# Compact state space tables in five parts and a held latent normalization in a two-layer hybrid decoder trunk

## The chip, the cores and the metric

The kernel runs on one core of a Trainium2 chip. The metric is the device time of one execution in microseconds (us); lower is better. PE is TensorE (matmul), DVE is VectorE, ACT is ScalarE, POOL is GpSimd, and SP is SyncE, whose queue issues nearly all DMAs.

## The reference, cut to what matters

Two layers work on one sequence of 256 tokens with 1024 features, in float32. Each layer runs three token mixers on the same input x and joins them with gates: an RWKV-7 time mix, a latent attention (MLA), and a diagonal state space mixer (S5). Then come an output projection, a layer norm, a SwiGLU feed-forward network (FFN), and a second layer norm.

```python
p = x @ w_in[l]
y_a = rwkv7_time_mix(p[..., :o_mla], ...)
y_b = mla_branch(p[..., o_mla:o_s5], ...)
y_c = s5_branch(p[..., o_s5:o_gate], ...)
merged = gates[..., 0, :] * y_a + gates[..., 1, :] * y_b + gates[..., 2, :] * y_c
x = layer_norm(ALPHA * x + merged @ w_out[l], ...)
h = silu(x @ ffn_w1[l]) * (x @ ffn_w3[l])
x = layer_norm(ALPHA * x + h @ ffn_w2[l], ...)
```

Two pieces matter here. The S5 mixer has 32 groups with 64 complex states and 16 channels each. From `lambda` and `log_step` it derives a magnitude, a cosine and a sine per state, and multiplies the input matrices B by a complex factor f:

```python
mag, ang = jnp.exp(lam_re * step), lam_im * step
lb_re, lb_im = mag * jnp.cos(ang), mag * jnp.sin(ang)
bb_re = f_re[..., None] * br - f_im[..., None] * bi
bb_im = f_re[..., None] * bi + f_im[..., None] * br
```

The MLA branch normalizes two latent vectors (256 and 128 wide) by their root mean square before it projects them up.

## The kernel before, in words

**Weights.** There are 138 weight chunks of 128x1024 floats per layer, in the order in which they are used. For each chunk `w_load` issues one DMA on SP's queue into a ring of 3 buffers (`raw`), ACT casts it to the fp32r value `whi` (L161), and DVE subtracts to get the rest `wlo` (L171; a tail of some chunks is subtracted on POOL, L173). Each product is then three matmuls, `whi` with the high part of x, `whi` with its low part, `wlo` with the high part (L203 to L205). `w_next` runs four chunks ahead; `whi` and `wlo` have four buffers each.

**Order of the work.** `ORDER1` and `ORDER2` spell out each layer's mixer stage as tokens. In `ORDER1[0]`: `S0 S1` project the S5 input, `m` the MLA latents, `P` loads the layer's parameters, `r0` to `r6` are seven RWKV projections (`rw_unit`, two chunks and 48 matmuls each, with a shift of tokens in `mix_in`: ACT at L570, DVE at L571), `G1` to `G3` gates, `T0 T1 T2` the three parts of the state space tables, `N` the normalization of the latents (`mla_norm`), `t`/`w` the two halves of four S5 tiles, `g0 g1` their gelu. The tokens give the program order, which is a priority and not the order in which instructions are issued. When the program is built, a planner goes through it with its own costs: for each engine it takes, of the instructions that it reckons to be ready, the one that stands first in the program. So a late instruction that is ready early goes ahead of an earlier one. On the chip each engine and SP's queue then work strictly in the order so fixed.

**State space tables** (`s5_tables`, a generator; each token advances it to the next `yield`). First come the scalars of both layers (`s5scal`, on DVE with two sines on ACT). `exp_acc` computes an exponential by a polynomial with 24 instructions on 128x32 values, and is called twice, in a chain. Then:

- Part one loads B and C, padded with zeros to block diagonal 128x512 matrices by the host (two DMAs of 512 KB), and makes three complex products with `cmul` (L381 to L386, six 128x512 instructions each) and one negation (L394). In layer 0 all of it is on DVE, in layer 1 on POOL.
- Part two transposes `bd` on PE (L404) and makes the small matrix `k0` (L413).
- Part three is the rotation: cosine and sine tables `ct`, `st` for 128 steps, by doubling (L429 to L434), 48 instructions of 128x16 to 128x512, on POOL in both layers. It reads and writes SBUF alone.

The S5 tiles need all of it: `bl` for the matmul at L702, `ct` and `st` for DVE's L709 and L710, `m2` for the scans (L721), `k0` and `cd` for L735 to L747.

**Latents.** `mla_norm` takes squares on ACT with a sum (L624, L625), adds epsilon on DVE (L235), takes the power -0.5 on POOL (L237, tile `rsm`), scales `lt` on ACT (L630, L631), rotates a part on DVE (L635 to L638), transposes on PE (L643 to L649) and copies to `mlain` on ACT (L645, L650). Nothing reads `mlain` before token `U` of `ORDER2`. The copies of the S5 input `u` (L113) are on ACT too, and eight DMAs on SP's queue bring them to `U2` (L671).

**Layer 1's tables** are made during layer 0's FFN: the loop over f = 2..21 advances the generator at f in `TAB_AT = (7, 12, 17)`, in a temporary pool `tmp1`. After the last part the pool's memory goes to the layer norm's `lg`, `lb` and `xk`, whose loads (L493 to L495) stand on SP's queue among the weight loads.

Of the kernel before, what the change touches and what calls it, by code (L numbers as in the profile page):

```python
# [8 lines left out]
F32 = mybir.dt.float32  # L9
# [17 lines left out]
    "S0 m S1 P r0 T0 T1 r1 N T2 r2 t0 w0 r3 G3 t1 t2 w1 r4 r5 w2 t3 w3 g0 G1 r6 G2 g1",  # L27
# [6 lines left out]
TAB_AT = (7, 12, 17)  # L34
# [52 lines left out]
def trunk(ctx: ExitStack, tc: tile.TileContext, xT, xtok, ws, spA, spB, spC, sp5, lnv, cst, out, dbg=None,  # L87
# [112 lines left out]

    def mm3(ps, w, x, first, last):
# [67 lines left out]
    with tc.tile_pool(name="s5set", bufs=1) as q:  # L269
# [5 lines left out]
        def exp_acc(dst, src):  # L275
            xc, n, r, pl = t5("xc"), t5("n"), t5("r"), t5("pl")
            ni = t5("ni", I32)
            V.tensor_scalar(out=xc, in0=src, scalar1=-104.0, scalar2=88.7, op0=ALU.max, op1=ALU.min)
# [13 lines left out]
            V.tensor_tensor(out=dst, in0=pl, in1=ni.bitcast(F32), op=ALU.mult)  # L292
# [55 lines left out]
    def s5_tables(l, tab, tmp, G, E):  # L348
# [12 lines left out]
        pb = tmp.tile([128, 2, 8, 2, 32], F32, name="pb", tag="pb")  # L361
        SY.dma_start(out=pb, in_=spB[l, :, 0:1024].rearrange("p (r q a c) -> p r q a c", r=2, q=8, a=2))
# [25 lines left out]
        def B(i, ri):
            return bd[:, :, ri, :, i]

        cmul(B(1, 0), B(1, 1), s5fr[:, p0:p0 + 16], s5fi[:, p0:p0 + 16], pb[:, 0], pb[:, 1])
        cmul(B(0, 0), B(0, 1), lr, li, B(1, 0), B(1, 1))

        G.tensor_scalar(out=cd[:, 1], in0=cd[:, 1], scalar1=-1.0, scalar2=None, op0=ALU.mult)  # L394
        G.tensor_scalar(out=li, in0=li, scalar1=-1.0, scalar2=None, op0=ALU.mult)
        cmul(cd[:, 2], cd[:, 3], lr, li, cd[:, 0], cd[:, 1])
# [123 lines left out]
    for l in range(layers):  # L520
# [136 lines left out]
        with tc.tile_pool(name=f"s5p{l}", bufs=1, side=P) as q:  # L657
# [17 lines left out]
            def s5_tables0(i):  # L675
# [4 lines left out]
                if i == 2:  # L680
                    tgen[0][0].close()
# [807 lines left out]
```

## Time and profile before

| | |
|---|---|
| time, median of 3 runs | 1086.61 us (1079.62 to 1089.05) |
| profiled execution | 1090.58 us, its span 1088.9 us |
| PE busy | 1026.9 us (94%) |
| DVE busy | 802.8 us (74%) |
| ACT busy | 477.3 us (44%) |
| POOL busy | 231.5 us (21%) |
| mean granted TensorE clock | 0.972 of full speed |

The trace is of one execution. Times are from the start of the span. The matmuls' ends are modelled, so a PE that is shown busy need not be at its peak. In a list of instructions a line gives start, duration, engine, line, operation and tile, and in brackets the idle time of the engine before it and what ended that.

### The profile page before, as it was taken

Reading aid. Unit: us, or ns where it says so; the run is one execution under the profiler, and the core shown is the slowest. Engines: PE = TensorE matmul, PEld = TensorE weight load, DVE = VectorE, ACT = ScalarE, POOL = GpSimd, SP = SyncE. Lnnn points to the kernel's source line nnn. Section 1 sums busy time; section 2 is a strip of 40 time slices with the busy share of each in tenths; the row PEclk is TensorE's granted clock in tenths of the full one; section 3 lists DMA queues with packets and bytes.
Section 4 is the critical chain, followed back from the end, with each engine's and each line's share of the span. In section 5 each row is a group of like instructions: output and inputs, shape, how many; then the busy total and the mean of one; then the engine's idle time right before and its main releaser. Section 6 shows DMA issues by size and latency. Waiting matters only on the chain.

```text
span 1088.9 us, 21216 instructions
## 1 busy us (share of the span) xinstructions
PE 1026.9 (94%) x8560; PEld 923.8 (85%) x8560; DVE 802.8 (74%) x1560; ACT 477.3 (44%) x789; POOL 231.5 (21%) x254
## 2 busy tenths in 40 slices
PE   9489999999999999899998999999999899999997
PEld 8378887888897899798878999878889779999985
DVE  7599988977478799576473898789756866676645
ACT  5243387544343344244325345765334433434331
POOL 2941042210000599400011003221002420000000
PEclk9789999999999999999998899999999999999999
DMA  7342262132285655466545325222225746555552
GB/s 279 98 140 86 95 192 73 59 118 96 81 291 183 204 173 167 178 209 217 184 143 177 115 80 173 90 97 79 79 98 169 243 152 230 186 183 180 186 195 78
DMA packets 47683, 164.91 MB, mean 151 GB/s; under 512 B 5729, under 2 KB 8289, under 8 KB 46689
## 3 DMA queue, kind: packets, MB, share of 16 engines
q1 hardware_dynamic: 47296, 163.03, 45.2%
q8 instruction: 67, 1.10, 0.4%
q10 hardware_dynamic: 288, 0.52, 0.1%
q14 instruction: 32, 0.25, 0.1%
HBM read 157.77 MB, written 4.19 MB: 149 GB/s over the span
## 4 chain that ended last, share of the span: by engine, by line
PE 61%; DVE 17%; POOL 10%; DMA 5%; ACT 3%; issue 3%; SPq 0%; DVEq 0%; ACTq 0%; POOLq 0%
PE mm L205 11%; PE mm L204 11%; PE mm L203 11%; DMA raw<-in_ws 4%; PE mm L488 3%; PE mm L489 3%; PE mm L487 3%; DVE wlo L171 3%; ACT whi L161 2%; DVE z L721 2%; POOL st L432 1%; POOL st L434 1%; PE pa L702 1%; POOL t L430 1%; PE pa L916 1%
## 5 line engine op out<-in xcount | busy, mean ns | idle before, releaser
L171 DVE TENSOR_TENSOR wlo<-raw,whi 128x1024 fp32r<-128x1024 f32 (+2 forms) x265 | 336.7, 1277 | 175.3 <-ACT whi L161 173.2
L161 ACT CAST whi<-raw 128x1024 fp32r<-128x1024 f32 (+2 forms) x267 | 277.5, 1043 | 386.0 <-PE mm L204 207.3
L203 PE MATMUL mm<-xh,whi 128*128 128x256 f32 x1312 | 379.5, 289 | 14.2 <-ACT whi L161 14.1
L205 PE MATMUL mm<-xh,wlo 128*128 128x256 f32 x1312 | 378.3, 289 | 2.1 <-DVE wlo L171 1.9
L204 PE MATMUL mm<-xl,whi 128*128 128x256 f32 x1312 | 379.3, 289 | 0.4 <-DVE xl L259 0.4
L203 PEld LDWEIGHTS mm<-xh,whi 128*128 128x128 f32 x1312 | 252.5, 192 | 18.7 <-ACT whi L161 14.7
L205 PEld LDWEIGHTS mm<-xh,wlo 128*128 128x128 f32 x1312 | 253.5, 193 | 6.1 <-DVE wlo L171 2.9
L204 PEld LDWEIGHTS mm<-xl,whi 128*128 128x128 f32 x1312 | 252.4, 192 | 3.9 <-issue 1.8
L237 POOL TENSOR_TENSOR rs<-rs,mhalf 128x1 f32<-128x1 f32 x8 | 7.8, 970 | 344.0 <-DVE rs L235 344.0
L203 PE MATMUL mm<-yh,whi 128*128 128x256 f32 x256 | 74.5, 291 | 0.1
L205 PE MATMUL mm<-yh,wlo 128*128 128x256 f32 x256 | 74.1, 290 | 0.0
L204 PE MATMUL mm<-yl,whi 128*128 128x256 f32 x256 | 74.1, 289 | 0.0
L488 PE MATMUL mm<-wlo,hh 128*128 128x512 f32 x132 | 52.0, 394 | 0.0
L487 PE MATMUL mm<-whi,hh 128*128 128x512 f32 x132 | 51.6, 394 | 0.0
L489 PE MATMUL mm<-whi,hl 128*128 128x512 f32 x132 | 51.5, 393 | 0.0
L203 PEld LDWEIGHTS mm<-yh,whi 128*128 128x128 f32 x256 | 48.5, 189 | 2.3 <-ACT qa L113 0.9
L204 PEld LDWEIGHTS mm<-yl,whi 128*128 128x128 f32 x256 | 48.5, 189 | 1.2 <-issue 0.8
L205 PEld LDWEIGHTS mm<-yh,wlo 128*128 128x128 f32 x256 | 48.6, 190 | 1.1 <-issue 0.7
L173 POOL TENSOR_TENSOR wlo<-raw,whi 128x384 fp32r<-128x384 f32 (+2 forms) x24 | 29.5, 1236 | 72.4 <-ACT whi L161 72.4
L237 POOL TENSOR_TENSOR rsn<-rsn,mhalf 128x8 f32<-128x8 f32 x4 | 6.5, 1634 | 142.8 <-DVE rsn L235 142.8
L923 POOL TENSOR_SCALAR_AFFINE_SELECT Mk<-Mk 64x512 f32<-64x512 f32 x32 | 27.0, 844 | 43.6 <-ACT Mk L113 42.3
L487 PEld LDWEIGHTS mm<-whi,hh 128*128 128x128 f32 x132 | 24.8, 188 | 6.1 <-DVE th L1260 0.7
(498 smaller groups left out, 1764.2 us busy)
## 6 DMA issues: line engine op xcount, KB each, us to landing
raw<-in_ws SPq DMA_DIRECT2D x267, 512.0 KB, 4.1
raw<-in_ws SPq DMA_DIRECT2D x8, 416.0 KB, 3.5
xd<-xk SPq DMA_DIRECT2D x3, 1024.0 KB, 4.1
xk<-xd SPq DMA_DIRECT2D x3, 1024.0 KB, 7.9
lg<-in_lnv SPq DMA_DIRECT2D x4, 512.0 KB, 5.1
lb<-in_lnv SPq DMA_DIRECT2D x4, 512.0 KB, 5.7
pc<-in_spC SPq DMA_DIRECT2D x2, 768.0 KB, 5.1
pb<-in_spB SPq DMA_DIRECT2D x2, 512.0 KB, 5.2
```

Source lines behind the costliest of these rows:

```text
L161: S.copy(out=hi[:, s], in_=raw[:, s])
L171: V.tensor_tensor(out=lo[:, 0:m], in0=raw[:, 0:m], in1=hi[:, 0:m].bitcast(F32), op=ALU.subtract)
L173: G.tensor_tensor(out=lo[:, m:w], in0=raw[:, m:w], in1=hi[:, m:w].bitcast(F32), op=ALU.subtract)
L203: PE.matmul(ps, lhsT=wh, rhs=xh, start=first, stop=False)
L204: PE.matmul(ps, lhsT=wh, rhs=xl, start=False, stop=False)
L205: PE.matmul(ps, lhsT=wl, rhs=xh, start=False, stop=last)
L237: G.tensor_tensor(out=out, in0=in_, in1=mh(out), op=ALU.pow)
L487: PE.matmul(acc[b][n], lhsT=ah, rhs=w[0][:, s], start=(k == 0), stop=False)
L488: PE.matmul(acc[b][n], lhsT=ah, rhs=w[1][:, s], start=False, stop=False)
L489: PE.matmul(acc[b][n], lhsT=al, rhs=w[0][:, s], start=False, stop=(k == nk - 1))
L721: V.tensor_tensor_scan(out=z[:, pp, qq, ri], data0=bc(m2[:, j:j + 1], [128, 128]), data1=z[:, pp, qq, ri], initial=0.0, op0=ALU.mult, op1= ...
L923: G.affine_select(out=Mk[r, h], in_=Mk[r, h], pattern=[[0, 4], [1, 2], [1, 64]], compare_op=ALU.is_ge, fill=0.0, base=-1, channel_multipli ...
```

## The change

The host no longer pads B and C; one DMA of 512 KB brings all four compact matrices. `cmul` works on them in place with 128x256 instructions, two at a time on separate scratch tiles, and a new step `spread` writes the padded form with two instructions of 128x512 output each (mask columns `g0`, `g1`): on ACT in layer 0, on POOL in layer 1. There are four spreads, so eight such instructions per layer. In layer 0 the tables come in five parts, the rotation first, and the tokens move: the products that need the tables go behind `r3`, the normalization `N` goes behind `r5`, and an order on ScalarE keeps its four squares behind the last `mix_in` activation traced before it, that of `r5`. In layer 1 the parts are advanced at f = 7, 8, 9, 12, 17, the rotation last. `exp_acc` needs 15 instructions in place of 24.

```diff
-    "S0 m S1 P r0 T0 T1 r1 N T2 r2 t0 w0 r3 G3 t1 t2 w1 r4 r5 w2 t3 w3 g0 G1 r6 G2 g1",
+    "S0 m S1 P r0 T0 T1 r1 T2 T3 r2 r3 T4 G3 t0 w0 r4 t1 r5 N w1 t2 w2 r6 t3 w3 g0 G1 G2 g1",
-TAB_AT = (7, 12, 17)
+TAB_AT = (7, 8, 9, 12, 17)
...
-            V.tensor_scalar(out=n, in0=n, scalar1=MAGIC, scalar2=None, op0=ALU.subtract)
-            V.tensor_scalar(out=n, in0=n, scalar1=-127.0, scalar2=127.0, op0=ALU.max, op1=ALU.min)
+            V.tensor_scalar(out=n, in0=n, scalar1=MAGIC + 127.0, scalar2=MAGIC, op0=ALU.min, op1=ALU.subtract)
...
-            for k in range(6, -1, -1):
-                V.tensor_tensor(out=pl, in0=pl, in1=r, op=ALU.mult)
-                V.tensor_scalar(out=pl, in0=pl, scalar1=co[k], scalar2=None, op0=ALU.add)
+            for k in range(7, 0, -1):
+                V.scalar_tensor_tensor(out=pl, in0=pl, scalar=co[k], in1=r, op0=ALU.add, op1=ALU.mult)
...
-        SY.dma_start(out=pb, in_=spB[l, :, 0:1024].rearrange("p (r q a c) -> p r q a c", r=2, q=8, a=2))
+        SY.dma_start(out=pb, in_=spB[l].rearrange("p (r q a c) -> p r q a c", r=4, q=8, a=2))
...
+        if first:
+            rotation()
+            yield
+        bt, bs = (tmp.tile([128, 8, 2, 16], F32, name=n, tag=n) for n in ("bt", "bs"))
...
+        def cmul(x, fr, fi):
+            fr, fi = (bc(v2(t, 8).unsqueeze(3), [128, 8, 2, 16]) for t in (fr, fi))
+            G.tensor_tensor(out=bs, in0=x[:, 0], in1=fi, op=ALU.mult)
+            G.tensor_tensor(out=bt, in0=x[:, 1], in1=fi, op=ALU.mult)
+            G.tensor_tensor(out=x[:, 0], in0=x[:, 0], in1=fr, op=ALU.mult)
+            G.tensor_tensor(out=x[:, 1], in0=x[:, 1], in1=fr, op=ALU.mult)
+            G.tensor_tensor(out=x[:, 0], in0=x[:, 0], in1=bt, op=ALU.subtract)
+            G.tensor_tensor(out=x[:, 1], in0=x[:, 1], in1=bs, op=ALU.add)
+        def spread(dst, src):
+            for g in range(2):
+                o, i = dst[:, :, 16 * g:16 * g + 16], src.rearrange("p r q a c -> p (r q a) c")
+                if l:
+                    G.tensor_scalar(out=o, in0=i, scalar1=C(f"g{g}"), scalar2=None, op0=ALU.mult)
+                else:
+                    S.activation(out=o, in_=i, func=AF.Identity, scale=C(f"g{g}"))
+        cmul(pb[:, 0:2], s5fr[:, p0:p0 + 16], s5fi[:, p0:p0 + 16])
+        spread(bdv[:, :, 1], pb[:, 0:2])
+        G.tensor_scalar(out=pb[:, 3], in0=pb[:, 3], scalar1=-1.0, scalar2=None, op0=ALU.mult)
+        spread(cd[:, 0:2].rearrange("p r q a c -> p (r q a) c"), pb[:, 2:4])
+        yield
+        cmul(pb[:, 0:2], lr, li)
+        spread(bdv[:, :, 0], pb[:, 0:2])
+        yield
+        G.tensor_scalar(out=li, in0=li, scalar1=-1.0, scalar2=None, op0=ALU.mult)
+        cmul(pb[:, 2:4], lr, li)
+        spread(cd[:, 2:4].rearrange("p r q a c -> p (r q a) c"), pb[:, 2:4])
+        yield
...
-            S.activation(out=dst, in_=ps, func=AF.Identity, scale=omu[:, col:col + 1])
+            state["mix"] = S.activation(out=dst, in_=ps, func=AF.Identity, scale=omu[:, col:col + 1])
...
+            with tc.issue_after(inst(state["mix"])) if l == 0 else ExitStack():
+                for b in range(2):
+                    S.activation(out=sq, in_=lt[:, b, 0:256], func=AF.Square, scale=1.0 / 16, accum_out=ss[:, b, 0:1])
...
```

## Rows read from the trace of the kernel before

**Rows 1.** Busy time by stretches: PE, PEld, DVE, ACT, POOL, PEclk, DMA share, GB/s.
```profile
20.00:30.00 10.00, 9.61 (x66) 9.39 (x65) 9.86 (x55) 6.75 (x16) 5.96 (x13) 1.00 0.77 257
...
33.90:46.20 12.30, 3.09 (x26) 2.88 (x24) 0.29 (x2) 1.73 (x4) 11.83 (x18) 0.77 0.01 6
...
36.99:80.00 43.01, 22.26 (x200) 21.05 (x200) 32.70 (x32) 16.19 (x29) 30.23 (x24) 0.72 0.31 94
...
46.20:79.00 32.80, 21.26 (x188) 20.05 (x189) 32.51 (x31) 13.46 (x26) 21.27 (x14) 0.72 0.38 115
79.00:145.00 66.00, 62.85 (x705) 56.74 (x703) 62.79 (x125) 29.26 (x44) 11.12 (x9) 1.00 0.35 114
145.00:200.00 55.00, 54.33 (x381) 46.75 (x382) 46.21 (x138) 41.70 (x99) 13.72 (x21) 1.00 0.31 99
```

**Rows 2.** Waits of PE, 0 to 160 us: total, times, longest.
```profile
PE mm L203 <- ACT whi L161: 9.5, 2, 9.3
PE pb L413 <- DVE bd L383: 7.3, 1, 7.3
```

**Rows 3.** Instructions of ACT, of POOL and of DVE around the first wait.
```profile
44.47 0.51 ACT L630 ACTIVATE lt<-lt,rsm 128x256 f32<-128x256 f32 x1 [14.56 <-POOL rsm L237]
...
43.39 1.04 POOL L237 TENSOR_TENSOR rsm<-rsm,mhalf 128x4 f32<-128x4 f32 x1
...
46.23 1.66 DVE L171 TENSOR_TENSOR wlo<-raw,whi 128x1024 fp32r<-128x1024 f32 x1 [12.04 <-ACT whi L161]
```

**Rows 4.** Waits of SP's queue, in layer 0 and in layer 1: total, times, longest.
```profile
SPq L671 <- ACT lt L630: 17.0, 1, 17.0
...
SPq L493 <- POOL st L434: 12.1, 1, 12.1
```

**Rows 5.** DVE instructions: a product beside the rotation, one alone, two 128x256 alone.
```profile
63.49 1.75 DVE L384 TENSOR_TENSOR bd<-bd,lr 128x512 f32<-128x512 f32 x1
...
71.89 0.68 DVE L382 TENSOR_TENSOR bt<-cd,li 128x512 f32<-128x512 f32 x1
...
99.82 0.42 DVE L711 TENSOR_TENSOR z<-pa__1092,pb__1093 128x256 f32<-128x256 f32 x1
100.15 0.42 DVE L712 TENSOR_TENSOR z<-pa__1092,pb__1093 128x256 f32<-128x256 f32 x1
```

**Rows 6.** POOL instructions of the rotation: one alone, and the same form beside DVE.
```profile
41.36 1.04 POOL L430 TENSOR_TENSOR t<-st 128x512 f32<-128x512 f32 x1
...
52.53 1.51 POOL L430 TENSOR_TENSOR t<-st 128x512 f32<-128x512 f32 x1
```

**Rows 7.** PE in layer 1: the gap behind SP's wait, and the clock after it.
```profile
460.12 0.46 PE L203 MATMUL mm<-xh,whi 128*128 128x256 f32 x1 [4.54 <-ACT whi L161]
...
460.00:468.00 8.00, 7.30 (x36) 7.01 (x37) 7.57 (x12) 4.25 (x7) 0.00 (x0) 0.57 0.53 178
```

**Rows 8.** Busy time of DVE and POOL where both work, after that wait.
```profile
46.80:67.90 21.10, 9.61 (x107) 8.59 (x106) 21.10 (x17) 5.14 (x9) 20.67 (x14) 0.66 0.33 100
```

**Rows 9.** ACT: an Identity of 128x512 between SBUF tiles.
```profile
135.60 0.72 ACT L762 ACTIVATE ga<-ga,ones 128x512 f32<-128x512 f32 x1
```

**Rows 10.** DVE groups, 10 to 34 us (mean ns of one after the comma): half of the polynomial of `exp_acc`.
```profile
L289 DVE TENSOR_TENSOR t5pl<-t5pl,t5r 128x32 f32<-128x32 f32 x14 | 2.8, 197 | 0.2
```

**Rows 11.** POOL in layer 1: 128x256 steps (first, last), products (first, last), rotation's end, negation.
```profile
380.14 0.61 POOL L429 TENSOR_TENSOR ct<-ct 128x256 f32<-128x256 f32 x1
...
382.80 1.10 POOL L381 TENSOR_TENSOR bd<-pb,s5fr 128x512 f32<-128x512 f32 x1
...
414.33 1.73 POOL L434 TENSOR_TENSOR st<-st,t 128x256 f32<-128x256 f32 x1
...
419.12 1.47 POOL L386 TENSOR_TENSOR cd<-cd,bt 128x512 f32<-128x512 f32 x1
...
447.12 2.15 POOL L434 TENSOR_TENSOR st<-st,t 128x512 f32<-128x512 f32 x1
...
L394 POOL TENSOR_SCALAR cd<-cd 128x512 f32<-128x512 f32 x1 | 1.5, 1547 | 0.0
```

More of the change, by code (lines that the diff above doesn't have):

```diff
@@ L346, in step, with s5_tables @@
             next(g)
-    def s5_tables(l, tab, tmp, G, E):
+    def s5_tables(l, tab, tmp, G, E, first):
         mark("s5pre")
@@ L388, in B, with rotation @@
[L388 to L394, printed above, removed]
+        def rotation():
+            mark("s5pre")
+            t2 = tmp.tile([128, 16, 32], F32, name="t2", tag="t2")
+            n = 1
+            while n < 128:
+                w = min(n, 32)
+                lc, ls = (bc(x[:, :, n - 1:n], [128, 16, w]) for x in (ct, st))
+                for o in range(0, n, w):
+                    c0, s0, t = ct[:, :, o:o + w], st[:, :, o:o + w], t2[:, :, 0:w]
+                    c1, s1 = ct[:, :, n + o:n + o + w], st[:, :, n + o:n + o + w]
+                    E.tensor_tensor(out=c1, in0=c0, in1=lc, op=ALU.mult)
+                    E.tensor_tensor(out=t, in0=s0, in1=ls, op=ALU.mult)
+                    E.tensor_tensor(out=c1, in0=c1, in1=t, op=ALU.subtract)
+                    E.tensor_tensor(out=s1, in0=c0, in1=ls, op=ALU.mult)
+                    E.tensor_tensor(out=t, in0=s0, in1=lc, op=ALU.mult)
+                    E.tensor_tensor(out=s1, in0=s1, in1=t, op=ALU.add)
+                n *= 2
@@ L412, in s5_tables @@
             for ri in range(2):
[L413 removed]
+                PE.matmul(o, lhsT=bd[:, ri, qx, pp, 1], rhs=cd[:, ri, qx, pp], start=(ri == 0), stop=(ri == 1),
                           skip_group_check=True)
@@ L417, in s5_tables @@
             cp(1, out=k0[r], in_=v2(ps[r, 0:256], 8))
-        yield
-        mark("s5pre")
-        t2 = tmp.tile([128, 16, 32], F32, name="t2", tag="t2")
-        n = 1
-        while n < 128:
-            w = min(n, 32)
-            lc, ls = (bc(x[:, :, n - 1:n], [128, 16, w]) for x in (ct, st))
-            for o in range(0, n, w):
-                c0, s0, t = ct[:, :, o:o + w], st[:, :, o:o + w], t2[:, :, 0:w]
-                c1, s1 = ct[:, :, n + o:n + o + w], st[:, :, n + o:n + o + w]
-                E.tensor_tensor(out=c1, in0=c0, in1=lc, op=ALU.mult)
-                E.tensor_tensor(out=t, in0=s0, in1=ls, op=ALU.mult)
-                E.tensor_tensor(out=c1, in0=c1, in1=t, op=ALU.subtract)
-                E.tensor_tensor(out=s1, in0=c0, in1=ls, op=ALU.mult)
-                E.tensor_tensor(out=t, in0=s0, in1=lc, op=ALU.mult)
-                E.tensor_tensor(out=s1, in0=s1, in1=t, op=ALU.add)
-            n *= 2
+        if not first:
+            yield
+            rotation()
         tb.update(ct=ct, st=st, m2=m2, cd=cd, bl=bl, k0=k0)
@@ L622, in mla_norm @@
             ss = q.tile([128, 2, 2], F32, name="ssm", tag="ssm")
-            for b in range(2):
-                S.activation(out=sq, in_=lt[:, b, 0:256], func=AF.Square, scale=1.0 / 16, accum_out=ss[:, b, 0:1])
-                S.activation(out=sq[:, 0:128], in_=lt[:, b, 256:384], func=AF.Square, scale=128.0 ** -0.5,
-                             accum_out=ss[:, b, 1:2])
+            with tc.issue_after(inst(state["mix"])) if l == 0 else ExitStack():
+                for b in range(2):
+                    S.activation(out=sq, in_=lt[:, b, 0:256], func=AF.Square, scale=1.0 / 16, accum_out=ss[:, b, 0:1])
+                    S.activation(out=sq[:, 0:128], in_=lt[:, b, 256:384], func=AF.Square, scale=128.0 ** -0.5,
+                                 accum_out=ss[:, b, 1:2])
             rs = q.tile([128, 2, 2], F32, name="rsm", tag="rsm")
@@ L1439, in cb @@
             return a.reshape(16, 2, 16, 64).transpose(1, 3, 0, 2).reshape(128, 16, 16)
-        def diag(a):
-            o = np.zeros((2, 64, 16, 2, 16), np.float32)
-            for i in range(2):
-                o[i, :, :, i, :] = a.reshape(2, 64, 16, 16)[i]
-            return o.reshape(128, 512)
         cr, ci = cb(g["s5_c_re"][l]), cb(g["s5_c_im"][l])
-        spB.append(np.concatenate([diag(a) for a in (br, bi, cr, ci)], 1))
+        spB.append(np.concatenate([a.reshape(128, 256) for a in (br, bi, cr, ci)], 1))
     lre = np.concatenate([pg_(g["s5_lambda_re"][l]) for l in range(nl)], 1)
```

40 lines of the change are left out of this document (16 added, 24 removed).

## The prediction

> **What bounds the kernel now.** I read the page first: PE is busy 94% of the span at a mean clock of 0.972, so a gain has to be found where PE stands still or where its clock is low. Then the table of stretches, to find those places [rows 1]. Between 37 and 80 us PE has 22.26 us of work in 43 us at a clock of 0.72: about half of this stretch is lost. Next, PE's waits in this stage [rows 2]: 9.3 us for a weight cast on ACT, then 7.3 us for a product of the tables on DVE. Last, the instructions around the first of them [rows 3]. ACT stands 14.56 us in front of the latent scaling L630, for the power on POOL; POOL has only this one step of 1.04 us to give, but it stands in the middle of the rotation, in an order fixed when the program was built. ACT's casts stand behind it, so DVE waits 12.04 us for a cast and PE 9.3 us. SP's queue is caught as well: the S5 input's eight DMAs wait 17.0 us for ACT, with weight loads behind them [rows 4]. So the first loss is an order problem on ACT and POOL.
>
> After it, DVE decides. From 46.2 to 79 us it is busy 32.51 of 32.80 us, and from 79 to 145 us 62.79 of 66 [rows 1]; PE's 62.85 in the latter is near it but is partly modelled. From 145 us on PE is the bound, 54.33 of 55. And DVE is slow because POOL works beside it: a product of 128x512 takes 1.75 us beside the rotation and 0.68 us alone [rows 5], and a POOL step goes from 1.04 to 1.51 [rows 6]. In layer 1 a smaller loss stands at 455 to 468 us: SP's queue waits 12.1 us in front of the layer norm's load for the rotation to release the pool [rows 4], PE then stands 4.54 us and runs at a clock of 0.57, a mixture of 1.2 and 2.4 GHz, for 8 us [rows 7].
>
> **The change part by part, layer 0.** All terms are for the time at which DVE has finished the first mixer stage, since DVE is what the stage ends on.
>
> *The normalization moved behind `r5`.* DVE's wait of 12.04 us goes. But in that wait POOL ran the rotation alone: in 33.9 to 46.2 us DVE was busy 0.29 us and POOL 11.83 [rows 1], 10.8 without the power, and some 0.6 more until 46.8. This work now falls beside DVE's, and I have to price that. In 46.8 to 67.9 us both engines are busy throughout [rows 8]. What they did there is, at the prices of the instructions when alone, on POOL 13 steps of 1.04, 13.5 us [rows 6]; on DVE 12 instructions of the products at 0.59 (0.68 less the 0.09 by which neighbours overlap: two of 128x256 that take 0.42 start 0.33 apart), a weight split at twice that and about 0.9 of small ones, 9.2 us [rows 5]. Together 22.7 us of work in 21.1 us of time: they hardly overlap, a factor of 1.08. DVE lost 21.1 - 9.2 = 11.9 us to POOL there. After the change POOL has 11.4 + 13.5 = 24.9 us to do beside a DVE that always has something: by the same ratio (9.2 to 13.5) DVE does 17.0 us meanwhile, in (24.9 + 17.0) / 1.08 = 38.8 us, and loses 21.8. Before it lost 12.04 + 11.9 = 23.9. So of the wait that goes, only 2.1 us are a gain. Bounds: -23.9 if the new overlap cost nothing, +1.0 if the two never overlapped (41.9 - 17.0 = 24.9 lost). I take -2.1, the factor that the row shows.
>
> The Trainium skill (SBUF — State Buffer, section "SBUF: two separate sides") holds that a DVE instruction with two SBUF inputs and a GpSimd instruction exclude each other for the whole instruction. The row is 8% short of that; by the rule the term would be +1.0 and not -2.1.
>
> What is queued behind the new order on ACT: the casts and shifts of `r6` and later. The four squares still lead to an addition on DVE, the power on POOL and four scalings on ACT, and ACT will again stand there until the power is done. By then the rotation is over, so that is POOL's 1.04 us [rows 3] and DVE's backlog. Bounds 0 to the old 14.56; I take 0, as casts run up to four chunks ahead and DVE is the later of the two. Nothing reads the latents before `U`, several tens of us on.
>
> *Smaller products.* Eighteen products and a negation go from 128x512 to 128x256: 0.59 to 0.33 us each on DVE [rows 5], 19 x 0.26 = 4.9 us less. Bounds: 0, if beside POOL the waiting and not the size sets the time, and -10, if the excess (1.75 against 0.68) halves too.
>
> *Eight spreads on ACT.* 8 x 0.72 = 5.8 us [rows 9] on an engine that has 13.46 us of work in 32.8 [rows 1]. Hidden, at 0; but each waits for a group of products on DVE with weight casts behind it, and if every spread is handed to DVE as waiting it costs all 5.8.
>
> *Shorter exponentials.* Two calls, nine instructions fewer each, 18 x 0.197 = 3.5 us [rows 10] on a DVE that is busy 9.86 of 10 us there [rows 1], and in a chain in front of both the rotation and the first product. I take -3.0; bounds 0 and -3.5. PE is not short of work at that time, but DVE's queue starts earlier on what decides later.
>
> *The tables' products behind `r3`, the DMAs.* PE no longer stands in front of the tables' small matmuls [rows 2] before `r1` to `r3`; it does `r3` and `G3` early. These are 96 of the 705 matmuls of 79 to 145 us, so there PE's 62.85 us fall by a seventh to about 54, below DVE's 62.79: DVE remains the bound and the gain so far passes on, into a stage bound by PE. The removed half MB per layer is 0 (PE had weights at that time; a gain is bounded by the few us of one transfer), and the eight DMAs of the S5 input are now issued earlier, in front of weights that PE wants later: 0, at most 2 us.
>
> Sum in layer 0: -2.1 - 4.9 - 3.0 = -10.0 us.
>
> **Layer 1.** POOL's stream ends at 449.3 [rows 11], and SP's queue with it. Eighteen products are at a mean of 1.71 us now (18 from the first row to the last, 1.10 to 2.27) and the negation at 1.55, 32.3 us. Rotation steps of 128x256 in the same stretch are six, from 0.61 to 1.73, mean 1.01: 18 x 1.01 + 1.0 for the negation = 19.2. No spread was on POOL; the nearest row is the negation, 1.55, with one tensor input as a spread has: 8 x 1.55 = 12.4. Together 31.6, 0.7 us less. So the spreads eat what the products give, and the wait on SP stays nearly whole: -0.7. Bounds: 0.61 each for all 26 and a negation, 16.5 us, ends 16 us earlier and takes away the whole gap of 4.54 us and most of the slow clock behind it (8 us at 0.57, 3.4 us), -8; for the other bound see the last rival.
>
> Total -10.7. The profiled execution took 1090.58 us, which becomes 1079.9; it lies 4.0 above the median of the runs shown, 1086.61, from which the same sum gives 1075.9.
>
> **Rivals.** *PE gets its loss back.* If POOL's steps fall between DVE's (a shift out of PSUM, waits for ACT) so that only half of the 21.8 us are lost, 10.9 us more are gained: 1065.0, and with layer 1's gap gone 1057. For it speaks that PE loses half of 43 us; against it that in 46.8 to 67.9 no such gaps were found. *The lock is full.* The term of +1.0, by the skill's rule above; 1079.0, within 1%. For it: a factor of 1.08 is near 1; against it: the row. *POOL's stream grows.* Slower. A step beside DVE can cost its waiting and not its size: 1.73 us for 128x256 [rows 11]. If all 19 small ones cost that and the spreads as much as the dearest step there, 2.15, the stream is 32.9 + 17.2 = 50.1 us, 17.8 longer. SP's queue then stands 17.8 us longer in front of the layer norm's load, PE's gap grows by as much, and -10.0 + 17.8 = +7.8 gives 1094.4. It makes the kernel slower from a growth of 10.0 us on, a mean of 1.57 us over the 27 instructions. Against it: four of six such steps took under 0.8. Beside these, the order itself: the planner may put the squares or the rotation where ACT stands just as long. The change then gives only the smaller DVE work, -8, in reach of no change.
>
> **How the numbers follow.** The forecast of 1075.9 has a chance of 0.52, with a range of its own from 1070 to 1082; a measurement tells about 1% (10.9 us) from no change, so the forecast lies on that bound: 0.27 of it faster, 0.25 the same. PE gets its loss back: 0.20, faster. The full lock: 0.12, the same. The old order in a new place: 0.05, the same. POOL's stream grows: 0.11, 0.10 of it slower and 0.01 the same. Faster 0.47, same 0.43, slower 0.10. The range goes from 1062 to 1090: below it the further half of the first rival, above it the slower rival.
>
> **What would show it.** Right: no wait of ACT over 3 us for POOL before 80 us; DVE busy over 95% from 32 us to the stage's end, which comes 10 us earlier; the rotation ending near 70 us and not at 68; products of 128x256 at 0.6 to 1.0 us beside POOL; SP's wait at L493 of 9 to 13 us, POOL ending at 447 to 450. Wrong: PE busy without gaps in 37 to 70 us (the first rival), ACT waiting for POOL or for products over 10 us in all, or POOL ending after 455 us.

## The result and the profile after

The changed kernel takes 1072.5 us (median of 4 runs, 1069.0 to 1078.0) against 1086.3 of the kernel before in the same measurement (4 runs): a ratio of 0.9881, 95% interval [0.9846, 0.9917]. The prediction was 1075.9 us. The profiled execution took 1068.97 us, with a span of 1067.1; it lies 3.5 us under the median, and the profile of before (1090.58 us, its span 1088.9) 4.3 us over its own, so the two spans lie 21.8 us apart where the medians lie 13.8 apart. I therefore took a second pair of profiles on one chip (spans of 1084.6 us for the kernel before and 1072.6 for the changed one), and read the differences from both.

Five POOL instructions mark the same places of the program in every version: the power of layer 0's latents (`rsm`), the first copy of layer 1's tables (`lr`, at the start of layer 0's FFN: it waits for the FFN's first matmuls), the power of the layer norm behind that FFN (`rs`), the power of layer 1's latents (`rsm`) and the clearing of `n` after layer 1's first mixer stage. The timeline of POOL before (start, duration):

```profile
43.39 1.04 POOL L237 TENSOR_TENSOR rsm<-rsm,mhalf 128x4 f32<-128x4 f32 x1
...
367.57 0.40 POOL L359 COPY lr<-xh 128x16 f32<-128x16 f32 x1 [10.51 <-PE mm L1272]
...
575.90 1.74 POOL L237 TENSOR_TENSOR rsm<-rsm,mhalf 128x4 f32<-128x4 f32 x1 [1.16 <-issue]
...
671.08 0.40 POOL L807 MEMSET n<- 128x256 f32 x1 [3.53 <-issue]
```

And after:

```profile
99.91 1.08 POOL L240 TENSOR_TENSOR rsm<-rsm,mhalf 128x4 f32<-128x4 f32 x1 [24.03 <-DVE rsm L238]
...
359.28 0.51 POOL L359 COPY lr<-xh 128x16 f32<-128x16 f32 x1 [10.52 <-PE mm L1296]
...
567.51 1.73 POOL L240 TENSOR_TENSOR rsm<-rsm,mhalf 128x4 f32<-128x4 f32 x1 [1.17 <-issue]
...
654.79 0.40 POOL L831 MEMSET n<- 128x256 f32 x1 [3.53 <-issue]
```

With the same marks of the second pair (`lr` at 368.44 and 356.32, the first `rs` at 553.63 and 543.01; in the first pair 553.97 and 546.41) the difference falls into these parts, in us:

| part | first pair | second pair | predicted |
|---|---|---|---|
| layer 0 up to its FFN (to `lr`) | -8.3 | -12.1 | -10.0 |
| layer 0's FFN with layer 1's tables (`lr` to `rs`) | +0.7 | +1.5 | -0.7 |
| layer norm, layer 1's latents (`rs` to `rsm`) | -0.8 | -0.6 | 0 |
| layer 1's first mixer stage (`rsm` to `n`) | -7.9 | -0.4 | 0 |
| the rest | -5.5 | -0.4 | 0 |

Layer 0 up to its FFN gives about the 10 us that were forecast. The first pair's extra 13 us stand where the instruction order of the two kernels is the same, and are not there in the second pair: they are scatter between executions. Most of it is a clock that falls or doesn't, below.

Inside layer 0 the first stage looks different from what I described. Busy time by stretches, after (columns as in [rows 1]), first the stretches of [rows 1], then two of 10 us:

```profile
36.99:80.00 43.01, 34.95 (x310) 33.42 (x309) 30.36 (x34) 20.90 (x33) 35.48 (x28) 0.84 0.44 142
46.20:79.00 32.80, 25.21 (x230) 23.98 (x231) 20.15 (x20) 18.02 (x28) 26.51 (x19) 0.79 0.40 131
79.00:145.00 66.00, 58.82 (x649) 51.30 (x647) 61.87 (x130) 34.39 (x65) 13.26 (x13) 1.00 0.32 99
...
40.00:50.00 10.00, 5.73 (x47) 5.43 (x45) 8.63 (x10) 3.50 (x7) 9.76 (x10) 0.92 0.51 171
50.00:60.00 10.00, 7.83 (x40) 7.54 (x41) 7.04 (x7) 5.47 (x10) 10.00 (x7) 0.57 0.47 156
...
450.00:460.00 10.00, 6.00 (x33) 5.71 (x34) 6.28 (x11) 4.71 (x6) 0.00 (x0) 0.66 0.68 258
```

From 37 to 80 us PE has 34.95 us of work and not 22.26. DVE is no longer full there: 20.15 of 32.80 us from 46.2 to 79, where it had 32.51. It is full again from 80 us on. The waits, after: ACT and PE from 20 to 100 us, and, while layer 1's tables are made, PE and SP's queue (total, times, longest):

```profile
ACT kr__236 L593 <- DVE kr__236 L594: 5.2, 3, 3.0
ACT cd L418 <- DVE pb L408: 5.0, 1, 5.0
...
ACT bd L418 <- DVE pb L409: 4.1, 2, 2.6
...
PE mm L206 <- ACT whi L161: 5.6, 1, 5.6
...
PE mm L206 <- ACT whi L161: 6.8, 1, 6.8
...
SPq L516 <- POOL st L389: 15.5, 1, 15.5
```

The wait of 14.56 us for `rsm` [rows 3] is gone, and so is PE's of 9.3 us [rows 2] and SP's of 17.0 in front of the S5 input [rows 4]. In their place ACT stands 5.0 us in front of one spread and 4.1 us in front of two others, for the products that they read, and PE stands 5.6 us in front of a cast queued behind the first of these waits; PE then runs at a clock of 0.57 from 50 to 60 us. While layer 1's tables are made, the wait of SP's queue for the rotation has grown from 12.1 to 15.5 us [rows 4], and PE's gap from 4.54 to 6.83 [rows 7]. The cost of single instructions, after, by group (mean ns after the comma): DVE from 25 to 72 us, and POOL's spreads in layer 1:

```profile
L171 DVE TENSOR_TENSOR wlo<-raw,whi 128x1024 fp32r<-128x1024 f32 x12 | 18.7, 1565 | 2.3 <-ACT whi L161 2.3
L408 DVE TENSOR_TENSOR pb<-pb,bt 128x256 f32<-128x256 f32 x3 | 2.8, 948 | 0.0
L594 DVE SCALAR_TENSOR_TENSOR kr__236<-mm,pa,kr__236 128x255 f32<-128x255 f32 x6 | 2.8, 474 | 1.8 <-ACT kr__236 L593 1.8
...
L416 POOL TENSOR_SCALAR bd<-pb,c 128x512 f32<-128x512 f32 x4 | 8.6, 2161 | 0.0
L416 POOL TENSOR_SCALAR cd<-pb,c 128x512 f32<-128x512 f32 x4 | 7.0, 1770 | 0.0
```

### The profile page after: what moved, and what is told of

Same layout as the page of the kernel before. It is cut to its first block, busy times and chain, and to the rows that moved or that the text cites. A ratio compares the mean times of both kernels' runs of the same rounds, so it can differ in the third digit from the quotient of the medians.

```text
span 1067.1 us, 21219 instructions
## 1 busy us (share of the span) xinstructions
PE 1014.2 (95%) x8560; PEld 912.5 (86%) x8560; DVE 784.7 (74%) x1542; ACT 482.6 (45%) x797; POOL 235.2 (22%) x262
## 4 chain that ended last, share of the span: by engine, by line
PE 58%; DVE 17%; POOL 9%; DMA 7%; ACT 5%; issue 3%; SPq 0%; DVEq 0%; ACTq 0%; POOLq 0%
PE mm L208 11%; PE mm L207 10%; PE mm L206 10%; DMA raw<-in_ws 6%; DVE wlo L171 3%; PE mm L511 3%; PE mm L512 3%; PE mm L510 3%; ACT whi L161 3%; DVE z L745 1%; PE pa L726 1%; PE pb L1035 1%; POOL st L387 1%; PE pb L1043 1%; PE pa L940 1%
## 5 line engine op out<-in xcount | busy, mean ns | idle before, releaser
L206 PE MATMUL mm<-xh,whi 128*128 128x256 f32 x1312 | 376.9, 287 | 14.2 <-ACT whi L161 13.9
L207 PE MATMUL mm<-xl,whi 128*128 128x256 f32 x1312 | 375.1, 286 | 0.4 <-DVE xl L262 0.4
L206 PEld LDWEIGHTS mm<-xh,whi 128*128 128x128 f32 x1312 | 249.2, 190 | 18.6 <-ACT whi L161 14.5
L208 PEld LDWEIGHTS mm<-xh,wlo 128*128 128x128 f32 x1312 | 250.2, 191 | 7.6 <-DVE wlo L171 4.0
```

## The experiments

Twelve runs, in three groups of four on one chip each. Each ratio is to the kernel before as it ran in the same group; "against after" is the difference of that ratio to the 0.9886 of the changed kernel in the first group, times 1085 us. With the two intervals taken together such a difference is uncertain by 4.4 to 6.1 us either way, so those of `rot_dve`, `exp_old` and `ln_warm` can't be told from 0. `lr` is the mark above, at the start of layer 0's FFN, and the last column is the stretch from `rsm` to `n` in layer 1. (Nothing is read from the profiles of `ln_hold` and `exp_old`, executions of 4948 and 1085 us; `ln_warm` has the edit of `ln_hold` too and stands for it.)

| run | ratio, 95% interval | against after | `lr` | `rsm` to `n` |
|---|---|---|---|---|
| `e1_before` | 1.0005 [0.9984, 1.0026] | +12.9 | 368.4 | 94.6 |
| `e2_after` | 0.9886 [0.9855, 0.9918] | 0 | 356.3 | 94.2 |
| `e3_norm_alone` | 0.9951 [0.9924, 0.9979] | +7.1 | 364.0 | 93.6 |
| `e4_tables_alone` | 1.0050 [1.0024, 1.0077] | +17.8 | 375.6 | 93.3 |
| `rot_dve` | 0.9876 [0.9833, 0.9920] | -1.1 | 356.0 | 86.8 |
| `spread_dve` | 0.9972 [0.9947, 0.9997] | +9.3 | 366.9 | 93.6 |
| `old_products` | 0.9935 [0.9907, 0.9963] | +5.3 | 364.0 | 93.9 |
| `ln_hold` | 0.9812 [0.9765, 0.9859] | -8.0 | | |
| `no_hold` | 1.0031 [1.0000, 1.0061] | +15.7 | 372.1 | 87.9 |
| `exp_old` | 0.9915 [0.9881, 0.9949] | +3.1 | | |
| `ln_warm` | 0.9870 [0.9828, 0.9911] | -1.7 | 356.6 | 97.2 |
| `rot_ln_warm` | 0.9832 [0.9794, 0.9871] | -5.9 | 355.3 | 98.2 |

### The two kernels again, and each half of the change alone

`e1_before` and `e2_after` are the two kernels without an edit.

> The kernel before, unchanged. Theory: of the 21.8 us between the two profiled spans only 7.6 come from the change (8.3 gained up to 360 us, 0.7 lost in layer 1's tables); the rest, 8 us at 576 to 660 and 5 us at 825 to 887, comes from executions that differ, since the order of the instructions on all five engines is the same there. Then this profile shows PE's wait for the S5 input of layer 1 and its clock somewhere between the two cases, not always the low clock of the first profile. Rival: the later 13 us are a part of the change; then this profile shows a clock near 0.8 at 580 to 620 again and a span near 1089. Ratio to before 1.000 within half a per cent in both.

> The changed kernel, unchanged. Theory: in the medians 8 to 14 us less than before (ratio 0.987 to 0.993), the first 360 us of this profile 8 us shorter than of a profile of before taken beside it, the layer's later stages within what one kernel's executions differ by. Rival (the change also saves 8 us in layer 1's first stage): the wait for the S5 input stays under 3 us and the clock at 1.00 there, in every profile of this kernel.

Measured: the kernel before repeats itself within 0.3%, and the changed kernel its ratio, 0.9886 for 0.9881. `e1_before`'s profile has the low clock of the first one again (0.79 from 580 to 620 us), which its theory didn't expect, at a span of 1084.6. What decides is `e2_after`: its stretch from `rsm` to `n` takes 94.2 us and not 87.3, with a clock that falls, so the rival of `e2_after` fails and the 8 us of the first pair are not the change's.

`e3_norm_alone` is the kernel before, with the normalization behind `r5` and held, and the tables as they were:

```
-... r1 N T2 r2 t0 w0 r3 G3 t1 t2 w1 r4 r5 w2 ...
+... r1 T2 r2 t0 w0 r3 G3 t1 t2 w1 r4 r5 N w2 ...
...
+            state["mix"] = S.activation(out=dst, in_=ps, func=AF.Identity, scale=omu[:, col:col + 1])
...
+            with tc.issue_after(getattr(state["mix"], "ins", state["mix"])) if l == 0 else ExitStack():
```

> Only the latent normalization is moved behind r5 and held there, the tables stay as before. Theory (DVE decides, and the rotation that ran alone during its wait now runs beside it): ACT's 14.56 us wait is gone, the gain is 2 us, at most 4, as DVE is busy from 32 us on without a gap and the rotation ends later than 68 us. Rival (the wait was the loss): the whole of PE's 9.3 us is gained.

`e4_tables_alone` is the changed kernel with the normalization back behind `r1` and not held:

```
-... r1 T2 T3 r2 r3 T4 G3 t0 w0 r4 t1 r5 N w1 ...
+... r1 N T2 T3 r2 r3 T4 G3 t0 w0 r4 t1 r5 w1 ...
-            with tc.issue_after(inst(state["mix"])) if l == 0 else ExitStack():
+            if True:
```

> The changed kernel with the latent normalization back behind r1 and not held. Theory: the smaller products and shorter exponentials alone give 6 us of the 8.3 of the first stages, although ACT again stands 10 us or more for the power behind rotation steps on POOL. Rival (the wait was the loss): within 2 us of before, as ACT's wait and PE's gap of 9 us come back whole.

Measured: the held normalization alone is worth 5.3 us (2.3 to 8.2 by the interval), more than the 2 us of its theory and less than the rival's 9.3; the rotation ends at 74.83 us as the theory said, but DVE works 41.94 us from 32 to 79 us and not throughout. The tables alone cost 5.4 us (2.6 to 8.3), where the theory forecast a gain of 6 and the rival no change: both fail. The two together gain 12.4. So the change is not a sum of parts. The longest waits of ACT and of PE in `e4_tables_alone`, 20 to 100 us:

```profile
ACT lt L654 <- POOL rsm L240: 21.9, 1, 21.9
...
PE pb L667 <- ACT lt L654: 17.9, 2, 17.3
```

and, in its timeline of POOL, the step that ACT waits for, between two of the rotation:

```profile
56.98 1.07 POOL L388 TENSOR_TENSOR t<-st,ct 128x512 f32<-128x512 f32 x1
58.01 1.04 POOL L240 TENSOR_TENSOR rsm<-rsm,mhalf 128x4 f32<-128x4 f32 x1
59.02 1.26 POOL L389 TENSOR_TENSOR st<-st,t 128x512 f32<-128x512 f32 x1
```

With the rotation first, the power comes to stand behind 13 of the rotation's 18 steps of 128x512 on POOL, at 58.01 us and not at 43.39, and ACT stands 21.9 us and not 14.56. Fourteen of the smaller products and the negation are done by 42 us, and nobody is there to use them: PE stands 17.3 us for the scaled latents, and ACT's next weight cast comes at 67.72 us, behind the same wait.

### Without the order on ScalarE

```
-            with tc.issue_after(inst(state["mix"])) if l == 0 else ExitStack():
+            with ExitStack():
```

> The changed kernel without the order on ScalarE: the normalization of the latents stays behind r5 in the list, but its instructions are free to be placed earlier. The new streams put its first activations behind the second cast on ScalarE, its scalings before the second spread, and its power step on GpSimd ahead of the last six large steps of the rotation. Theory (the wait for GpSimd is what the order takes away; it comes back): ScalarE stands over 8 us for the power step before 80 us, TensorE behind it, and the time is 8 to 19 us above the changed kernel's, 1080 to 1091 us, as with the tables alone. The rival (the place in the list is enough, the wait is short): within 2 us of the changed kernel.

Measured: 15.7 us slower than the changed kernel, as expected, and 0.3% above the kernel before (0 to 0.6%). The place in the list is not enough. ACT's and PE's longest waits of this run, 20 to 100 us:

```profile
ACT lt L654 <- POOL rsm L240: 19.0, 1, 19.0
...
PE mm L206 <- ACT whi L161: 19.8, 1, 19.8
```

ACT again stands in front of the scaling L654, the casts stand behind it, and PE stands as long. This is the wait of [rows 3], longer. So it is the order on ScalarE that makes the rotation first affordable.

### The rotation on VectorE

```
-TE_ = "VG"
+TE_ = "VV"
```

> The changed kernel with one edit: layer 0's rotation of the state space tables on VectorE, as its products are. The prediction's theory (the two engines hinder each other nearly as much as a lock would: 24.9 us of rotation on GpSimd cost VectorE 21.8 us): on VectorE alone the same 42 steps take some 17 to 20 us, so the time comes within 3 us of the changed kernel's, 1070 to 1076 us, with single rotation steps of 128x512 at 0.4 to 0.6 us. The rival (the engines run side by side and the factor is small): the rotation's whole 17 to 20 us come on top, 1087 us and more.

Measured: 1.1 us faster than the changed kernel, no difference that can be told. The groups of DVE from 25 to 72 us in this run: splits, one of the six lines of the rotation (its 128x512 steps), products and shifts:

```profile
L171 DVE TENSOR_TENSOR wlo<-raw,whi 128x1024 fp32r<-128x1024 f32 x12 | 14.7, 1227 | 1.0 <-ACT whi L161 1.0
...
L594 DVE SCALAR_TENSOR_TENSOR kr__236<-mm,pa,kr__236 128x255 f32<-128x255 f32 x6 | 2.9, 484 | 0.0
L389 DVE TENSOR_TENSOR st<-st,t 128x512 f32<-128x512 f32 x3 | 2.1, 699 | 0.0
...
L408 DVE TENSOR_TENSOR pb<-pb,bt 128x256 f32<-128x256 f32 x3 | 1.3, 430 | 0.0
```

The rotation's steps of 128x512 take 0.70 us each and not the 0.4 to 0.6 expected. The run prices what POOL's rotation costs DVE in the changed kernel. Twelve splits take 14.7 us alone and 18.7 beside the rotation. A product of 128x256 takes 0.43 us alone and 0.95 (L408) beside it; over all 18, by their groups, 7.8 and 13.9 us. Together DVE loses 10.1 us. The shifts L594, which read PSUM, take 0.48 and 0.47 and lose nothing. On DVE itself the 48 steps have 20.4 us of busy time, 16 with the 0.09 us by which neighbours overlap taken off. So moving them there adds some 6 us to DVE, and yet layer 0 ends as early. The same stretches as above, in this run:

```profile
40.00:50.00 10.00, 8.91 (x127) 7.96 (x125) 10.00 (x21) 5.51 (x9) 0.00 (x0) 1.00 0.48 166
50.00:60.00 10.00, 8.72 (x59) 8.60 (x60) 10.00 (x21) 3.70 (x5) 0.00 (x0) 0.83 0.35 113
```

DVE is full, and PE has 17.63 us of work where it had 13.56, with its wait for a cast of ACT in 20 to 80 us down from 5.6 to 0.2 us. The time is as the theory said. Its reason (nearly a lock, so it makes no difference) is only part of it: DVE had room, and products that are not delayed spare ACT most of its waits (1.0 us is left in front of a spread). By the Trainium skill (SBUF — State Buffer, section "SBUF: two separate sides") a DVE instruction with two inputs in SBUF and a GpSimd instruction that reads SBUF shut each other out. The unchanged L594 and the products at 1.8 times their cost agree with it; what it costs DVE here is the 10.1 us above. An instruction with one input can be slowed as well: the negation L424 takes 0.28 us alone and 0.41 beside the rotation.

### The spreads on VectorE

```
-                    S.activation(out=o, in_=i, func=AF.Identity, scale=C(f"g{g}"))
+                    V.tensor_scalar(out=o, in0=i, scalar1=C(f"g{g}"), scalar2=None, op0=ALU.mult)
```

> The changed kernel with one edit: layer 0's eight spreads by the group masks on VectorE instead of ScalarE. The profile of the changed kernel shows VectorE not full from 40 to 80 us, ScalarE standing 5.0 and 4.1 us ahead of two spreads for the product that they read, and TensorE 5.6 us without work behind ScalarE, after which its granted clock is 0.57 for 10 us. Theory one (the handover between VectorE and ScalarE is what costs): both waits of ScalarE and TensorE's gap go, the end of layer 0's tables comes 3 to 8 us earlier, 1065 to 1070 us. Theory two (VectorE's work decides, as the prediction had it): eight operations of 0.4 to 0.7 us more on VectorE, 3 to 6 us slower, 1076 to 1079 us.

Measured: 9.3 us slower; theory one falls, theory two has the sign, and its 3 to 6 us lie under the measured size, the 6 within its uncertainty of 4.4 us. PE's longest wait of 20 to 80 us in this run:

```profile
PE mm L208 <- DVE wlo L171: 15.8, 2, 15.5
```

one of the two groups of spreads on DVE:

```profile
L418 DVE TENSOR_SCALAR bd<-pb,c 128x512 f32<-128x512 f32 x4 | 3.9, 990 | 0.0
```

and the stretch in which PE waits:

```profile
50.00:60.00 10.00, 0.00 (x0) 0.00 (x0) 9.96 (x9) 2.22 (x3) 9.92 (x9) 0.50 0.00 0
```

Eight spreads take 7.7 us on DVE beside the rotation (0.95 and 0.99 each). Four of them stand in DVE's order in front of a weight split, PE stands 15.5 us for that split and has no matmul from 50 to 60 us. With them stand ten products (from 40.85 to 58.49 us); in the changed kernel only five products are left between two splits there. So the edit moved products too, and the run prices the spreads on DVE together with the order that the planner then made. In that order ACT's waits in the changed kernel, 9.1 us in all, are the cheaper way.

### The full-size products in the new order

The tables and their loads as before (three parts, `TAB_AT` old), in

```
-    "S0 m S1 P r0 T0 T1 r1 T2 T3 r2 r3 T4 G3 t0 w0 r4 t1 r5 N w1 t2 w2 r6 t3 w3 g0 G1 G2 g1",
+    "S0 m S1 P r0 T0 r1 r2 r3 T1 T2 G3 t0 w0 r4 t1 r5 N w1 t2 w2 r6 t3 w3 g0 G1 G2 g1",
```

> The changed kernel with the full-size products and the loads of the kernel before, but the new order, the held normalization and the weighted sum in place kept; layer 1's tables are the old ones too, in three parts. The prediction's term for the smaller products is 4.9 us in layer 0, and the longer stream of GpSimd in layer 1 measured 1.1 us against it: the time should be about 4 us above the changed kernel's, 1075 to 1078 us. The rival (with the normalization held, VectorE has room between 40 and 80 us, and products there cost nothing): within 1.5 us of the changed kernel or faster by the 1 us of layer 1.

Measured: 5.3 us slower than the changed kernel. `lr` comes at 364.0, 4.7 and 7.6 us after the two profiles of it; layer 1's tables take 185.6 us from `lr` to `rs` and not 187.1 and 186.7, 1.3 us back. The time is the expected one: the compact products with their spreads are worth some 6 us in layer 0. But it isn't DVE's work alone. The rotation is again the last part in this program, and beside the larger products it ends at 77.09 us, where it ended at 70.99. Its last step here and in the changed kernel:

```profile
75.81 1.28 POOL L431 TENSOR_TENSOR st<-st,t 128x512 f32<-128x512 f32 x1
...
69.71 1.28 POOL L389 TENSOR_TENSOR st<-st,t 128x512 f32<-128x512 f32 x1
```

POOL works without a gap in both from 24 us on, so its steps took longer, and DVE then stands 1.7 us for the last table.

### The old exponential

`exp_acc` as in the kernel before (nine instructions more in each of two calls); all else as changed. Its middle part:

```
-            for k in range(7, 0, -1):
-                V.scalar_tensor_tensor(out=pl, in0=pl, scalar=co[k], in1=r, op0=ALU.add, op1=ALU.mult)
+            for k in range(6, -1, -1):
+                V.tensor_tensor(out=pl, in0=pl, in1=r, op=ALU.mult)
+                V.tensor_scalar(out=pl, in0=pl, scalar1=co[k], scalar2=None, op0=ALU.add)
...
```

> The changed kernel with the old two-step evaluation of the exponential (more and shorter VectorE steps before 28 us), all else as changed. The prediction's term: 3.0 us on VectorE ahead of layer 0's products, on the path: the time comes 2 to 4 us above the changed kernel's. The rival (VectorE waits for ScalarE's casts in that stretch anyway, or has room behind it at 48 to 80 us): under 1.5 us.

Measured: 3.1 us slower in the medians, in the expected 2 to 4; with an uncertainty of 5.0 us the run doesn't tell it from the rival's 1.5 or from nothing.

### Layer 1's wait on SyncE

```
-            SY.dma_start(out=raw[:, s], in_=ws[i, :, s])
+            state["raw"] = SY.dma_start(out=raw[:, s], in_=ws[i, :, s])
...
+                with tc.issue_after(inst(state["raw"])) if ln == 2 and l == 0 else ExitStack():
+                    SY.dma_start(out=lg, in_=lnv[l, ln:ln + 1, :].to_broadcast([128, D]))
+                    SY.dma_start(out=lb, in_=lnv[l, ln + 1:ln + 2, :].to_broadcast([128, D]))
+                    SY.dma_start(out=xk, in_=x_dram)
```

> The changed kernel with one edit: on SyncE the three loads of layer 0's second normalization (its gain, its offset and the residual) stand behind the last raw weight load of that stretch, so that their wait for a buffer that GpSimd holds until its tables end (15.5 us in the changed kernel, 12.1 before) no longer stands ahead of weight loads. Theory one: TensorE's gap of 6.8 us at 454 us and the low clock behind it go, 6 to 11 us faster than the changed kernel, 1062 to 1067 us. Theory two (the gap is met by another wait right behind it): under 2 us.

Measured: 8.0 us faster than the changed kernel (uncertain by 6.1), 1064.3 us, 20 us under the kernel before: theory one. The three loads no longer stand ahead of weight loads, and what they cost can be seen in the next run, which has the same edit. In it the stretch of the gap looks like this:

```profile
440.00:450.00 10.00, 10.00 (x86) 10.00 (x85) 8.17 (x12) 4.05 (x6) 0.93 (x1) 1.00 0.61 200
450.00:460.00 10.00, 10.00 (x85) 10.00 (x85) 6.40 (x10) 4.42 (x6) 0.00 (x0) 1.00 0.57 195
...
570.00:580.00 10.00, 10.00 (x44) 8.58 (x43) 2.94 (x5) 1.05 (x1) 0.00 (x0) 0.56 0.29 82
```

PE is busy throughout at full clock from 440 to 460 us, where the changed kernel has 6.00 us of work at a clock of 0.66 in the second ten; from `lr` to `rs` it takes 177.3 us in place of 187.1 and 186.7. So the gap and the clock behind it cost some 9.6 us.

### Matmuls ahead of the reload of U

In layer 1 PE waits for `U` (in the kernel `U2`), the S5 input that DMAs bring back to SBUF. `ln_warm` is `ln_hold` with these lines in addition, and `rot_ln_warm` has `TE_ = "VV"` as well.

```
+                    if l and F == 0 and pp == 0:
+                        for i in range(16):
+                            PE.matmul(ps[:, 0:128], lhsT=bl[0:64, 0, 0, :], rhs=bl[0:64, 1, 0, :], start=True, stop=True)
```

> The changed kernel with the three loads of the second normalization held behind the last raw load, as before, and 16 matmuls of 128 columns (some 2.4 us, their output overwritten) ahead of layer 1's first state space products, where TensorE stands 2.3 to 4.0 us for the reload of U. In seven of the nine profiles so far the granted clock falls to 0.5 for some 12 us behind that wait, and the stretch from layer 1's normalization to the clearing of its state takes 114 to 117 us in place of 108. Theory (the wait itself brings the clock down): the granted clock stays 1.00 there and that stretch takes 108 us; the time comes 4 to 7 us below that of the held loads alone (ratio to before some 0.977), with a smaller spread. The rival (the clock falls for another reason, such as what ran before): no gain, or 1 to 2 us lost. In either case the profile should show TensorE's gap at 454 us and the clock of 0.57 behind it gone.

> The same as the run with the held loads and the 16 matmuls, with layer 0's rotation on VectorE in addition: the version that the runs so far point to. On its own the rotation on VectorE was worth 1 us at most against the changed kernel; expected 1055 to 1063 us, within 3 us of the run without it.

Measured: 6.3 us slower than `ln_hold`; with the rotation on DVE in addition 2.1 us slower. Neither difference is clear of its uncertainty (6.8 and 6.6 us). The theory's forecast of 4 to 7 us less fails, and the run doesn't test it as meant. `rot_ln_warm` took 1064.8 us, above the expected 1055 to 1063. PE's timeline in `ln_warm` (fillers, then the first product on U):

```profile
563.07 3.83 PE L727 MATMUL pa<-bl 64*128 64x128 f32 x32
...
569.46 0.68 PE L730 MATMUL pa<-U,bl 64*128 64x128 f32 x4 [2.24 <-DMA U<-u]
```

The 16 fillers ran as 32 passes at 563 us, right ahead of the wait and not in it. They cost 3.8 us, the wait of 2.24 us stayed, and behind it the clock was 0.56 in the mean (570 to 580 us in the fence above). `ln_hold` has the lowest median of the study; its interval overlaps those of `rot_ln_warm` and `ln_warm`.

## Why the prediction was right, and where it was not

**The sum.** -10.7 us was forecast, and the medians lie 13.8 apart in the first measurement and 12.4 by the second ratio. Layer 0 up to its FFN gave -8.3 and -12.1 for -10.0, the stretch with layer 1's tables +0.7 and +1.5 for -0.7. The total is right, and in part by luck: by the terms the move of the normalization gives 2.1 us and all the rest 8.6, while alone the one gave 5.3 and the other cost 5.4. The step on the normalization was wrong. What the new order of the other tokens, priced at 0, is worth by itself was not run.

**The normalization and the contention (-2.1).** The step said that of 12.04 us of waiting only 2.1 are gained, since the rotation then falls beside "a DVE that always has something" and costs it 21.8 us. Two things were wrong. First, DVE did not always have something: it worked 20.15 of 32.80 us, and the rotation cost its splits and products 10.1 us and not 21.8. That is the first rival's condition (half of the loss), and its 10.9 us more would have been due. They didn't come. The room was not used: ACT stood 9.1 us for products, PE 5.6 us for ACT, and PE's clock went to 0.57. That these waits are the reason is read from the trace and not shown: in `rot_dve` they are nearly gone, but the rotation is moved too. The factor from [rows 8] is a reading of a stretch in which both engines are full, and the error was to carry it into one in which DVE would wait. (It is also a little low: of the 13 POOL steps that were priced at 1.04 us, five are of the two forms that take 1.25 or 1.26 alone, as the step L389 in `e4_tables_alone`, and four take 1.07, as L388. With 14.7 us for 13.5 the factor is 1.13 and the term -2.8.) Second, I priced the move against the old wait of 12.04 us. With the rotation first ACT's wait is 21.9 us and not 14.56 if the normalization stays where it was, so in the new kernel the held move is worth 17.8 us (15.7 for the order on ScalarE alone); in the old one it is worth 5.3. A term "removed wait" belongs to a kernel, and I took it from the kernel before without asking what the other edits make of it.

**Smaller products (-4.9).** Putting them back costs 5.3 us in all and some 6 in layer 0, so the size is right; the mechanism was wider than DVE's own work, since POOL's rotation ended 6 us later too. In it lies the spreads' cost, which the prediction took as 0 and bounded by 5.8 "if every spread is handed to DVE as waiting". The waits were there, 9.1 us of ACT and 5.6 of PE; what they cost net was not measured on its own.

**Shorter exponentials (-3.0).** Putting the old ones back costs 3.1 us in the medians, with an uncertainty of 5.0: not contradicted, and not shown.

**DVE remains the bound from 79 us.** It is busy 61.87 of 66 us, and PE's work falls from 62.85 to 58.82 us, not to 54. The busy shares agree with the step; no run tests it by itself.

**Layer 1 (-0.7).** The mechanism was right: POOL's spreads eat what the smaller products give. The term that was mis-sized is the spread: 1.55 us from the negation as the nearest row, measured 2.16 and 1.77, mean 1.97, which makes 15.7 us for eight and not 12.4; the eighteen products took 18.4 us for the 18.2 forecast. From `lr` on POOL's stream takes 83.5 us (359.28 to 442.78) and not 81.7 (367.57 to 449.27). It grew by 1.8 us, so the slower rival's mechanism is there, far below the 10 us from which it would have decided. (That rival took 2.15 us for the dearest step; the prediction's own range has 2.27, which makes its growth 18.7 us for 17.8.)

**What was to be seen.** Right: no wait of ACT for POOL before 80 us, the rotation's end at 70.99 us, products of 128x256 at 0.77 us in the mean beside POOL. Wrong: DVE over 95% busy from 32 us to the stage's end (61% from 46.2 to 79), SP's wait of 9 to 13 us (15.5), and POOL's end at 447 to 450 us (442.78, as layer 0 had become shorter). ACT's 9.1 us for products lie close under the 10 us that were named as a sign of being wrong.

**The scatter.** The prediction placed its number by the median of the runs shown, since the profile of before lay 4 us above it. The profile of after is itself the fastest of its four executions. In the changed kernel itself the stretch from `rsm` to `n` took 87.3 us once and 94.2 us once. Its windows from `rsm` on in the second profile (`e2_after`):

```profile
573.88:583.88 10.00, 6.95 (x43) 6.20 (x42) 2.45 (x2) 2.90 (x8) 0.00 (x0) 0.84 0.75 221
583.88:593.88 10.00, 10.00 (x43) 9.10 (x43) 6.50 (x12) 2.95 (x4) 0.00 (x0) 0.50 0.00 0
```

and in the first:

```profile
577.51:587.51 10.00, 7.74 (x57) 6.81 (x55) 3.71 (x5) 4.49 (x10) 0.00 (x0) 1.00 0.73 223
587.51:597.51 10.00, 10.00 (x82) 9.85 (x82) 9.32 (x20) 4.03 (x6) 0.00 (x0) 1.00 0.40 125
```

PE had stood 3.0 us for U in `e2_after` and 2.3 in the first profile; then it worked without a gap in both, 43 matmuls in 10 us at 1.2 GHz or 82 at 2.4 GHz.

## What to carry to other kernels

A wait that the profile shows is worth what it costs in the kernel that is left after the other edits: here one held move was worth 5 us in the old kernel and 18 in the new, and the other half of the change, without it, made the kernel slower. Run each half alone before adding them up. When a shared resource makes two engines slow, take its factor only for stretches in which both really have work, and look for the queue (here SyncE's three loads, 8 us) in which a cheap instruction with a late condition stands ahead of the loads that the bound engine lives on.

## What the runs showed of the hardware

The clock behind the reload of U is not decided by the kernel alone: it held at 1.00 in 3 of the 12 profiles that are read (the first of after, `rot_dve`, `no_hold`) and fell to 0.5 in the others, for 13 to 17 us, which made the stretch from `rsm` to `n` 6 to 8 us longer (93.3 to 95.2 us for 86.8 to 87.9, the runs with fillers left out). In the changed kernel it held once and fell once. The wait in front was 2.3, 1.3 and 3.1 us where it held and 2.0 to 4.0 us where it fell, so its length alone doesn't tell them apart; what does is open.

On GpSimd a multiplication of 128x512 by a value per partition takes 1.77 and 2.16 us in the mean while layer 1's tables are made (the two groups of L416), no less than the products of two tensors of that size had taken there (1.10 to 2.27, mean 1.71), and 2.7 times the 0.72 us of ScalarE [rows 9].
